# Four changes to where modulation products, first features and state products stand in a two-block transformer kernel

## The chip, the cores and the metric

One NeuronCore of a Trainium2 chip runs the whole program. The time is device microseconds of one execution. The profiler names the engines PE (TensorE matmul), PEld (its weight loads), DVE (VectorE), ACT (ScalarE), POOL (GpSimd) and SP (SyncE, which issues the DMAs). All engines work through their own queue in order. Everything is float32; a plain float32 product is two records on PE, a product of operands split in a high and a low part (fp32r) is one.

## The reference, cut to what matters

Two blocks of two layers each work on 512 tokens (256 of context, 256 latent) with 2048 features. Each layer begins with a modulation: a condition vector for the latent tokens and one for the context tokens goes through SiLU and a 2048 x 6144 matrix, which gives shift, scale and gate for every feature. The third layer holds a recurrent mixer (RWKV) with 16 heads of 64 in two directions.

```
shift, scale, gate = split(silu(c) @ mod_w[l] + mod_b[l], 3)      # for c and for c_ctx
h = norm(x) * (1 + scale) + shift
y = mixer(h)                # layer 1 sliding-window attention, 2 latent attention, 3 RWKV + pool, 4 attention
x = x + gate * y
# RWKV, per head, token by token:
sa = S @ a
S  = S * w + outer(sa, b) + outer(v, k)
y  = S @ r
```

## The kernel before

**Tiling.** Activations are kept with features on the partitions: 16 k-chunks of 128 features, 512 tokens wide. A layer's linear products stream weights through two buffers (`raw`, cut into `whi` and `wlo` by ACT and DVE, L323 and L324), and `mm3` multiplies each chunk three times (L352 to L354). The kernel text is Python that emits instructions; a scheduler then sets the order on each engine, by readiness as it reckons it and, among ready ones, by the place in the text. A block marked high priority goes ahead of all others as soon as it is ready.

**Modulation.** `mod_steps` (L244) is a generator that other work advances. One load is 1 MB: four k-chunks of 512 output features (`mraw`, L240). Its four products (L260, M = 32 columns of weights each) use four column strips of the array, `tile_position=(0, 32*j)`, and write four partition strips of one PSUM bank, `mv`; here they are called a group. There are 192 loads in all, 48 for each layer. After the last group of a batch ACT copies the bank (`ev`, L267), four products with a selection matrix add up the strips (L273), and DVE adds the bias (L279). For the first layer a batch is shift and scale of 512 features (8 loads), then all gates (16 loads); for the others a batch is 16 loads. `mod_open` sets how many load buffers there are: three in the stretches around the output projections and at the start, one inside the mixers (L706, L848, L977), so that there a load is issued only when the group before it has read the buffer.

**Start.** Two modulation loads are issued, then x in four DMAs (L1690); ACT squares, DVE sums them up (L1519 to L1523), PE and POOL make the inverse norm (`sums`, `spread`), and after the modulation of a group `scales` and `put_h` make four k-chunks of h. Between groups the key and value products of the first attention (`keys`, `values`) are advanced.

**Scan.** `rwkv` treats two heads at a time, one in each half of the partitions, in 8 chunks of 64 tokens; there are 16 such units. In each chunk, in one PSUM bank called `chain`: A times state (L1418), copy to `Rp` (L1421), Q times state (L1422), the inverse TT times `Rp` (L1428), copies into the state tile SV (L1429 DVE, L1430 ACT), BKs times SV (L1432), the new state (L1438, with SD from POOL), QB times SV added to Q's product (L1441), copy to y (L1444). A and Q lie in `AQ[:, c, 0]` and `AQ[:, c, 1]`, both heads side by side, and both are multiplied with both heads' states, 128 moving columns, of which half the products serve no one. Other units' preparation and the projections stand between these in PE's queue.

## Time and profile before

| | us |
|---|---|
| median of 3 runs (3293.38 to 3304.43) | 3296.71 |
| the profiled execution | 3288.34 |
| its span | 3286.3 |
| PE busy in the span | 3117.3 |
| DVE busy | 2101.0 |
| ACT busy | 1481.1 |

The table is read from the top: the profiled execution is 8.4 us under the median, and 2.0 us of it lie outside the span. PE is busy 95% of the span, the next engine 64%. A record's busy time overlaps with the next record's, so what one product costs in a full queue is the distance from its start to the next start, not its duration.

### The profile page before, as it was taken

Reading aid. Unit: us, or ns where it says so; the run is one execution under the profiler, and the core shown is the slowest. Engines: PE = TensorE matmul, PEld = TensorE weight load, DVE = VectorE, ACT = ScalarE, POOL = GpSimd, SP = SyncE. Lnnn points to the kernel's source line nnn. Section 1 sums busy time; section 2 is a strip of 40 time slices with the busy share of each in tenths; the row PEclk is TensorE's granted clock in tenths of the full one; section 3 lists DMA queues with packets and bytes.
Section 4 is the critical chain, followed back from the end, with each engine's and each line's share of the span. In section 5 each row is a group of like instructions: output and inputs, shape, how many; then the busy total and the mean of one; then the engine's idle time right before and its main releaser. Section 6 shows DMA issues by size and latency. Waiting matters only on the chain. (4 is left out here: it accounts for less than half of the span.)

```text
span 3286.3 us, 53227 instructions
## 1 busy us (share of the span) xinstructions
PE 3117.3 (95%) x19762; PEld 2397.2 (73%) x19762; DVE 2101.0 (64%) x4647; ACT 1481.1 (45%) x3233; POOL 351.2 (11%) x536
## 2 busy tenths in 40 slices
PE   5999999999988999999999999999999999899997
PEld 2567777767777788897776676666677768678897
DVE  2446454553376666666777788777787546857766
ACT  2424444442276666653334334333343323646664
POOL 0000000000001111000122222221121101200000
PEclk8999999999999999999999999999999999999999
DMA  8843444348654666766434433334434474543454
GB/s 303 309 165 135 139 137 157 125 174 290 234 165 142 226 208 226 253 228 211 126 98 133 124 125 116 111 103 149 126 109 154 168 253 130 172 140 129 143 180 153
DMA packets 270771, 556.07 MB, mean 169 GB/s; under 512 B 122928, under 2 KB 150704, under 8 KB 244912
## 3 DMA queue, kind: packets, MB, share of 16 engines
q1 hardware_dynamic: 270512, 552.68, 50.8%
q8 instruction: 155, 2.54, 0.3%
q14 instruction: 104, 0.85, 0.1%
HBM read 517.46 MB, written 35.13 MB: 168 GB/s over the span
## 5 line engine op out<-in xcount | busy, mean ns | idle before, releaser
L324 DVE TENSOR_TENSOR wlo<-raw,whi 128x512 fp32r<-128x512 f32 (+2 forms) x1000 | 660.3, 668 | 572.7 <-ACT whi L323 538.3
L352 PE MATMUL a<-hhi,whi 128*128 128x512 f32 (+1 forms) x2752 | 972.8, 355 | 16.6 <-ACT whi L323 11.9
L323 ACT CAST whi<-raw 128x512 fp32r<-128x512 f32 (+2 forms) x1000 | 593.0, 599 | 815.4 <-PE a L353 470.8
L353 PE MATMUL a<-hlo,whi 128*128 128x512 f32 (+1 forms) x2752 | 947.3, 345 | 0.0
L354 PE MATMUL a<-hhi,wlo 128*128 128x512 f32 (+1 forms) x2752 | 940.0, 347 | 4.5 <-DVE wlo L324 4.3
L352 PEld LDWEIGHTS a<-hhi,whi 128*128 128x128 f32 x2752 | 525.6, 191 | 145.2 <-issue 45.0
L354 PEld LDWEIGHTS a<-hhi,wlo 128*128 128x128 f32 x2752 | 522.6, 191 | 63.5 <-DVE wlo L324 10.2
L353 PEld LDWEIGHTS a<-hlo,whi 128*128 128x128 f32 x2752 | 526.3, 191 | 46.0 <-issue 2.2
L456 POOL TENSOR_TENSOR rs<-st,mhalf 128x4 f32<-128x4 f32 (+3 forms) x109 | 145.7, 1337 | 1683.3 <-DVE st L453 1666.3
L260 PE MATMUL mv<-mraw,cs 128*32 128x512 f32 x1536 | 258.3, 629 | 16.5 <-DMA mraw<-mod_w 16.2
L352 PE MATMUL a<-whi,hhi 128*128 128x512 f32 (+1 forms) x672 | 260.6, 398 | 13.4 <-ACT sq L613 5.9
L353 PE MATMUL a<-wlo,hhi 128*128 128x512 f32 (+1 forms) x672 | 262.7, 391 | 1.4 <-DVE wlo L324 1.1
L354 PE MATMUL a<-whi,hlo 128*128 128x512 f32 (+1 forms) x672 | 258.8, 388 | 0.0
L1427 POOL TENSOR_SCALAR SD<-SV,DL 64x64 f32<-64x64 f32 x224 | 130.0, 580 | 468.7 <-DVE SV L1438 452.4
L352 PEld LDWEIGHTS a<-whi,hhi 128*128 128x128 f32 x672 | 126.1, 190 | 71.2 <-issue 18.6
L353 PEld LDWEIGHTS a<-wlo,hhi 128*128 128x128 f32 x672 | 127.9, 190 | 31.5 <-DVE wlo L324 7.3
L354 PEld LDWEIGHTS a<-whi,hlo 128*128 128x128 f32 x672 | 127.6, 190 | 25.4 <-issue 0.8
L565 ACT ACTIVATE pr<-sc,nm 128x512 f32<-128x512 f32 (+1 forms) x128 | 81.1, 633 | 90.2 <-DVE nm L562 66.7
L1430 ACT COPY SV<-chain 64x64 f32<-64x64 f32 x128 | 26.6, 208 | 184.5 <-DVE SV L1429 178.8
L556 DVE TENSOR_REDUCE mx<-sc 128x1 f32<-128x512 f32 (+1 forms) x128 | 78.9, 617 | 37.8 <-PE sc L766 15.9
L260 PEld LDWEIGHTS mv<-mraw,cs 128*32 128x32 f32 x1536 | 37.0, 110 | 87.8 <-issue 50.3
L1444 ACT COPY y<-chain 64x64 f32<-64x64 f32 x256 | 52.9, 207 | 98.2 <-PE chain L1441 87.8
(379 smaller groups left out, 4690.6 us busy)
## 6 DMA issues: line engine op xcount, KB each, us to landing
mraw<-mod_w SPq DMA_DIRECT2D x192, 1024.0 KB, 4.9
raw<-od_in SPq DMA_DIRECT2D x88, 512.0 KB, 3.6
raw<-swa_in SPq DMA_DIRECT2D x72, 512.0 KB, 3.6
raw<-ev_rkv SPq DMA_DIRECT2D x64, 384.0 KB, 3.4
raw<-ev_in SPq DMA_DIRECT2D x48, 512.0 KB, 3.9
raw<-swa_out SPq DMA_DIRECT2D x40, 512.0 KB, 5.6
raw<-ev_out SPq DMA_DIRECT2D x40, 512.0 KB, 3.6
raw<-mla_g SPq DMA_DIRECT2D x64, 256.0 KB, 3.3
```

What stands on the lines that cost most here:

```text
L260: nc.tensor.matmul(pb[32 * j : 32 * j + 32, :], cs[:, 32 * k + 30 - 2 * n : 32 * k + 62 - 2 * n], raw[:, j, :], start=(n == 0 and q == 0), ...
L323: nc.scalar.copy(whi, raw)
L324: nc.vector.tensor_tensor(wlo, raw, whi.bitcast(F32), op=ALU.subtract)
L352: mm(out, ah, bh, start=first, stop=False, skip_group_check=shared)
L353: mm(out, ah, bl, start=False, stop=False, skip_group_check=shared)
L354: mm(out, al, bh, start=False, stop=last, skip_group_check=shared)
L456: self.nc.gpsimd.tensor_tensor(dst, stv, mv, op=ALU.pow)
L556: nc.vector.reduce_max(mx, sc, axis=AX.X)
L565: nc.scalar.activation(pr[:, :n], sc, AF.Exp, scale=scale, bias=nm, accum_out=sm)
L1427: nc.gpsimd.tensor_scalar(SD[r_], SV[r_, hh, c, :], DL[r_, c : c + 1], None, ALU.mult)
L1430: nc.scalar.copy(SV[half[1], 1, c, :], ps[half[1], P : P + L])
L1444: nc.scalar.copy(y[r_, c, :], blk(3 * P, hh))
```

## The change

Four parts. **(1) First layer in halves.** The modulation of the first layer's shifts and scales goes by 256 features in place of 512: a load is still 1 MB, now eight k-chunks of 256 features from a second layout of the weights, `mod_h`, and it takes eight products of 256 columns, two in each strip. A batch is four such loads in place of eight; `scales`, `put_h` and the key products follow each half, the values each second. At the start x is loaded first, then three modulation loads. **(2) Priority.** The products of a load stand in a high-priority block, for all 192 loads. **(3) Products per head.** `AQ[:, c, hh]` now holds A of one head and Q of that head, in swapped places for the second head, so that one product of 64 moving columns with its own head's state gives both. L1418 and L1422 (128 columns each) become two products of 64 columns, both ahead of the copy to `Rp`. QB, the mask and the final copies change places to match. **(4)** Even and odd chunks use two different column ranges of the bank `chain`; SD has one buffer in place of two.

```diff
@@ modulation
+MOD_FIRST = tuple(((g, u), (4 + g, u)) for g in range(4) for u in range(2)) + ((8, 9, 10, 11),)
+MOD_BATCHES = (0, 4, 1, 5), (2, 6, 3, 7), (8, 9, 10, 11)
...
-            self.nc.sync.dma_start(out=raw, in_=self.I["mod_w"][i, g, q])
+            if isinstance(g, tuple):
+                raw = raw.rearrange("p k (a c) -> p (k a) c", a=2)
+                self.nc.sync.dma_start(out=raw, in_=self.I["mod_h"][g[0], g[1], q])
+            else:
+                self.nc.sync.dma_start(out=raw, in_=self.I["mod_w"][i, g, q])
...
+                nq, nk, cols = (2, 8, 256) if half else (4, 4, 512)
...
-                        for j in range(4):
-                            k = 4 * q + j
-                            nc.tensor.matmul(
-                                pb[32 * j : 32 * j + 32, :], cs[:, 32 * k + 30 - 2 * n : 32 * k + 62 - 2 * n], raw[:, j, :],
-                                start=(n == 0 and q == 0), stop=(n == len(gs) - 1 and q == 3), tile_position=(0, 32 * j),
-                            )
+                        with self.tc.high_priority():
+                            for kk in range(nk):
+                                k, j = nk * q + kk, kk % 4
+                                nc.tensor.matmul(
+                                    pb[32 * j : 32 * j + 32, :cols], cs[:, 32 * k + 30 - 2 * n : 32 * k + 62 - 2 * n],
+                                    raw[:, kk, :], start=(n == 0 and k < 4), stop=(n == len(gs) - 1 and k >= KD - 4),
+                                    tile_position=(0, 32 * j),
+                                )
@@ rwkv
-            nc.vector.scalar_tensor_tensor(AQ[r_, :, 0, hh, :], ch(kkn)[r_], -1.0, Dp[r_, :, 0:L], ALU.mult, ALU.mult)
+            nc.vector.scalar_tensor_tensor(AQ[r_, :, hh, hh, :], ch(kkn)[r_], -1.0, Dp[r_, :, 0:L], ALU.mult, ALU.mult)
...
-            mm(ps[:, 0:P], heads(AQ[:, c, 0]), SV[:, :, c, :], start=True, stop=True)
+            o = c % 2 * P
+            for hh in range(2):
+                out = ps[:, o + hh * L : o + hh * L + L]
+                mm(out, heads(AQ[:, c, hh]), SV[:, hh, c, :], start=hh == 0, stop=False, skip_group_check=True)
...
-            mm(ps[:, 3 * P :], heads(AQ[:, c, 1]), SV[:, :, c, :], start=False, stop=False, skip_group_check=True)
             if not last:
-                SD = ph.tile([P, L], F32, tag="SD", name=self.nm("SD"), bufs=2)
+                SD = ph.tile([P, L], F32, tag="SD", name=self.nm("SD"), bufs=1)
...
-            mm(ps[:, 3 * P :], heads(QB[:, c]), SV[:, :, c, :], start=False, stop=True, skip_group_check=True)
+            mm(ps[:, o : o + P], heads(QB[:, c]), SV[:, :, c, :], start=False, stop=True, skip_group_check=True)
@@ tile_network
-        N.mod_load()
-        N.mod_load()
         for k4 in range(0, KD, 4):
             nc.sync.dma_start(out=x[k4 // 4], in_=I["x"][:, k4 : k4 + 4, :])
...
+        for _ in range(3):
+            N.mod_load()
...
-        for g in range(4):
+        for g, u in ((g, u) for g in range(4) for u in range(2)):
...
-            todo += [values(g)] * 16 + [kgen] * 16 if VF and g == 3 else [kgen] * 16 + [values(g)] * 16
+            todo += [kgen] * 8
+            if u:
+                todo += [values(g)] * 16
```

What it moves in the order that the scheduler sets is shown at three places on PE. In the changed kernel the lines are numbered 10 to 18 higher: groups are L270, `mm3` is L366 to L368, and the scan's products are L1437 (A and Q), L1446 (TT), L1450 (BKs) and L1459 (QB).

The start of the program on PE, before: `mv` with x4 is a group, L273 the adding up, `a` the key products. Ahead of these rows stand the inverse norm (`sums`, `spread`) and the first six groups.

```order
L260 MATMUL mv_188<-mraw_217,cs_185 32x512 x4
L260 MATMUL mv_188<-mraw_223,cs_185 32x512 x4
L273 MATMUL mv_38_237<-sel,ev_235 128x4 x4
L260 MATMUL mv_293<-mraw_229,cs_185 32x512 x4
L352 MATMUL a_274<-whi_280,hhi 128x512
L353 MATMUL a_274<-wlo_281,hhi 128x512
L352 MATMUL a_275<-whi_280,hhi 128x512
L353 MATMUL a_275<-wlo_281,hhi 128x512
```

The same place after, from the first group on (`spread` is the inverse norm, L284 the adding up):

```order
L270 MATMUL mv_190<-mraw_159,cs_187 32x256 x8
L488 MATMUL spread_174<-ident,rs_170 128x128 x2
L270 MATMUL mv_190<-mraw_161,cs_187 32x256 x8
L488 MATMUL spread_174<-ident,rs_170 128x128
L270 MATMUL mv_190<-mraw_163,cs_187 32x256 x8
L270 MATMUL mv_190<-mraw_207,cs_187 32x256 x8
L284 MATMUL mv_34_229<-sel,ev_227 128x4 x2
L270 MATMUL mv_269<-mraw_217,cs_187 32x256 x8
L366 MATMUL a_250<-whi_256,hhi 128x512
```

Moved: the adding up comes after four loads in place of eight, the first key product after five in place of nine, and the first groups stand among the transposes of `spread`. Behind these rows come 10 more key products, the sixth load's group, 10 more, and the seventh's; then the eighth's to eleventh's come with only 3 key products among them, ahead of the third k-chunk's products.

A chunk of the scan on PE, before, where a group is cut: one product of the load ahead of the chain's A product, three behind it.

```order
L1441 MATMUL chain_19159<-SV_18662,qb_14957 128x128
L260 MATMUL mv_17059<-mraw_19446,cs_9283 32x512
L1418 MATMUL chain_19159<-SV_18662,AQ_18258 128x128
L260 MATMUL mv_17059<-mraw_19446,cs_9283 32x512 x3
L352 MATMUL a_19063<-hhi,whi_19575 128x512
L353 MATMUL a_19063<-hlo,whi_19575 128x512
L354 MATMUL a_19063<-hhi,wlo_19576 128x512
L1422 MATMUL chain_19159<-SV_18662,AQ_18258 128x128
L1428 MATMUL chain_19159<-Rp_19490,tt 128x64
```

A chunk of the scan after: the four products of a load are one row (x4), and A and Q are two products of 64 columns that stand next to each other.

```order
L1437 MATMUL chain_21953<-SV_21456,AQ_21050 128x64 x2
L478 MATMUL sums_22213<-c_bsel,sq_22211 128x2 x4
L270 MATMUL mv_21434<-mraw_23186,cs_9552 32x512 x4
L1446 MATMUL chain_21953<-Rp_22168,tt 128x64
L366 MATMUL a_21857<-hhi,whi_22224 128x512
L367 MATMUL a_21857<-hlo,whi_22224 128x512
L368 MATMUL a_21857<-hhi,wlo_22225 128x512
L1450 MATMUL chain_21953<-SV_21456,BKs_21406 128x128
```

Moved: nothing stands between the products of a load, and nothing of the chain stands between `Rp` and TT. In the whole order before, 42 of the 192 groups are cut, 28 of them in the scan's layer; after, none is (160 rows with x4, 32 with x8).

What the chain's products wait for, before (`waits` names the engine whose semaphore it is):

```order
L1418 MATMUL chain_15808<-SV_15412,AQ_15210 128x128 [waits Activation_49]
L1280 MATMUL bon_15876<-r_15676,c_bones 128x512 [waits DVE_49,PE_49]
L352 MATMUL a_15573<-hhi,whi_15887 128x512
L1422 MATMUL chain_15808<-SV_15412,AQ_15210 128x128 [waits DVE_49]
L1428 MATMUL chain_15808<-Rp_15860,tt 128x64
L353 MATMUL a_15573<-hlo,whi_15887 128x512
L354 MATMUL a_15573<-hhi,wlo_15888 128x512
```

And after:

```order
L1459 MATMUL chain_15962<-SV_15566,qb_15110 128x128 [waits DVE_49]
L1295 MATMUL bon_16030<-r_15830,c_bones 128x512 [waits PE_49]
L1437 MATMUL chain_15962<-SV_15566,AQ_15364 128x64 [waits Activation_49]
L1437 MATMUL chain_15962<-SV_15566,AQ_15364 128x64
L366 MATMUL a_15727<-hhi,whi_16041 128x512
L367 MATMUL a_15727<-hlo,whi_16041 128x512
L368 MATMUL a_15727<-hhi,wlo_16042 128x512
L366 MATMUL a_15728<-hhi,whi_16041 128x512
L367 MATMUL a_15728<-hlo,whi_16041 128x512
L1446 MATMUL chain_15962<-Rp_16015,tt 128x64 [waits DVE_49]
```

Moved: the Q product is gone from between; the first product of a chunk waits for ACT as before.

## Rows read from the trace of the kernel before

**Rows 1.** The page: the span and how busy each engine is.

```profile
span 3286.3 us, 53227 instructions
PE 3117.3 (95%) x19762; PEld 2397.2 (73%) x19762; DVE 2101.0 (64%) x4647; ACT 1481.1 (45%) x3233; POOL 351.2 (11%) x536
```

**Rows 2.** Stretches: busy us of PE, PEld, DVE, ACT, POOL; then clock, DMA share, GB/s.

```profile
0.00:56.00 56.00, 19.51 (x92) 6.39 (x92) 16.09 (x30) 16.08 (x29) 2.19 (x8) 0.87 0.82 316
56.00:190.00 134.00, 129.71 (x647) 81.13 (x648) 57.84 (x111) 49.40 (x92) 2.03 (x2) 0.98 0.74 270
...
1460.00:2640.00 1180.00, 1140.48 (x7961) 814.35 (x7960) 881.35 (x2028) 446.67 (x1105) 234.71 (x416) 0.99 0.43 134
```

**Rows 3.** Instructions in order of time, start of the program: start us, us, engine, line.

```profile
25.97 1.83 PE L464 MATMUL sums<-ones,acc 128*128 128x2 f32 x8 [25.97 <-DVE acc L1523]
...
30.60 4.69 PE L260 MATMUL mv<-mraw,cs 128*32 128x512 f32 x24
...
48.89 1.94 PE L260 MATMUL mv<-mraw,cs 128*32 128x512 f32 x8 [2.17 <-DMA mraw<-mod_w]
...
56.33 0.80 PE L352 MATMUL a<-whi,hhi 128*128 128x512 f32 x1 [1.06 <-ACT hhi L498]
```

**Rows 4.** The same view, PE alone: a modulation group together, and one cut in two.

```profile
61.94 0.39 PE L353 MATMUL a<-wlo,hhi 128*128 128x512 f32 x1
62.17 0.40 PE L354 MATMUL a<-whi,hlo 128*128 128x512 f32 x1
62.49 1.07 PE L260 MATMUL mv<-mraw,cs 128*32 128x512 f32 x8
63.49 0.50 PE L352 MATMUL a<-whi,hhi 128*128 128x512 f32 x1
...
2000.31 1.05 PE L260 MATMUL mv<-mraw,cs 128*32 128x512 f32 x2
2001.29 0.49 PE L1418 MATMUL chain<-SV,AQ 128*128 128x128 f32 x2
2001.71 1.06 PE L260 MATMUL mv<-mraw,cs 128*32 128x512 f32 x6
2002.70 0.50 PE L352 MATMUL a<-hhi,whi 128*128 128x512 f32 x1
```

**Rows 5.** How long loads of modulation weights take, and what waits for them.

```profile
DMA to landing us min/median/max: 4.6/4.9/17.2
...
PE mv L260 <- DMA mraw<-mod_w: 8.8, 8, 4.1
```

**Rows 6.** PE in order of time, second attention: modulation groups close together.

```profile
1098.19 1.06 PE L260 MATMUL mv<-mraw,cs 128*32 128x512 f32 x8
1099.18 0.39 PE L352 MATMUL a<-hhi,whi 128*128 128x256 f32 x1
...
1104.25 1.07 PE L260 MATMUL mv<-mraw,cs 128*32 128x512 f32 x8
...
1259.50 0.38 PE L352 MATMUL a<-hhi,whi 128*128 128x256 f32 x1
...
1267.46 1.06 PE L260 MATMUL mv<-mraw,cs 128*32 128x512 f32 x8 [1.56 <-DMA mraw<-mod_w]
```

**Rows 7.** PE in order of time, inside the scan: products of 128, 64, 2 columns.

```profile
2003.50 0.38 PE L1422 MATMUL chain<-SV,AQ 128*128 128x128 f32 x2
2003.72 0.33 PE L1428 MATMUL chain<-Rp,tt 128*128 128x64 f32 x2
2003.86 0.48 PE L352 MATMUL a<-hhi,whi 128*128 128x512 f32 x1
...
2393.14 0.95 PE L464 MATMUL sums<-c_bsel,sq 128*128 128x2 f32 x8
2393.95 0.47 PE L352 MATMUL a<-hhi,whi 128*128 128x512 f32 x1
```

**Rows 8.** Who waits for whom in the scan, after 60 us: total us, times, longest us.

```profile
PEld chain L1418 <- ACT y L1444: 43.4, 86, 0.9
```

More of the change, by code (lines that the diff above doesn't have):

```diff
@@ L210, in modulation @@
         self.mod_done = set()
-        order = [(i, g) for i in range(4) for gs in MOD_BATCHES[min(i, 1)] for g in gs]
-        self.mod_loads = [(i, g, q) for i, g in order for q in range(4)]
+        order = [(i, g) for i in range(4) for gs in (MOD_BATCHES if i else MOD_FIRST) for g in gs]
+        self.mod_loads = [(i, g, q) for i, g in order for q in range(2 if isinstance(g, tuple) else 4)]
         self.mod_ahead, self.mod_pool, self.mod_wait = [], None, 0
@@ L248, in mod_steps @@
             mod, cs = self.mod[i], self.cs
-            for gs in MOD_BATCHES[min(i, 1)]:
+            for gs in MOD_BATCHES if i else MOD_FIRST:
                 pb = self.bank("mv")
+                half = isinstance(gs[0], tuple)
+                nq, nk, cols = (2, 8, 256) if half else (4, 4, 512)
                 for n, g in enumerate(gs):
-                    for q in range(4):
+                    for q in range(nq):
                         while len(self.mod_ahead) < (self.mod_pool[1] - 1 if self.mod_pool and self.mod_loads else 0):
@@ L270, in mod_steps @@
                 p2 = self.bank("mv2")
-                c = 2 * len(gs)
-                for j in range(4):
+                c, nb = 2 * len(gs), cols // P
+                for j in range(nb):
                     nc.tensor.matmul(
@@ L276, in mod_steps @@
                 for n, g in enumerate(gs):
-                    bias = self.v("mod_b", i * 48 + g * 4, 4).unsqueeze(2).broadcast_to([P, 4, 2])
-                    pv = p2[:, : 4 * c].rearrange("p (j n c) -> p j n c", j=4, c=2)[:, :, n, :]
-                    nc.vector.tensor_tensor(mod[:, g * 4 : (g + 1) * 4, :], pv, bias, op=ALU.add)
+                    o = g[0] * 4 + g[1] * 2 if half else g * 4
+                    bias = self.v("mod_b", i * 48 + o, nb).unsqueeze(2).broadcast_to([P, nb, 2])
+                    pv = p2[:, : nb * c].rearrange("p (j n c) -> p j n c", j=nb, c=2)[:, :, n, :]
+                    nc.vector.tensor_tensor(mod[:, o : o + nb, :], pv, bias, op=ALU.add)
                     self.mod_done.add((i, g))
+                    if half and g[1]:
+                        self.mod_done.add((i, g[0]))
                 yield
@@ L1088, in ev_consts @@
         nc.gpsimd.memset(self.smask[:, 0:NT:L], 0.0)
-        self.gmask = load("gmask", [P, P])
+        self.gmask = load("gmask", [P, 3 * L])
         self.m16 = load("m16", [P, 64])
@@ L1251, in rwkv @@
             r_ = half[hh]
[L1252 removed]
+            nc.vector.tensor_tensor(AQ[r_, :, hh, 1 - hh, :], ch(r)[r_], Dp[r_, :, 1:], op=ALU.mult)
         yield
@@ L1269, in rwkv @@
                     lhs = BK[r_, c, :, :].rearrange("p a t -> p (a t)")
-                    mm(pbs[hh][:, (c - c4) * P : (c - c4 + 1) * P], lhs, AQ[r_, c, :, hh, :], start=True, stop=True)
+                    mm(pbs[hh][:, (c - c4) * P : (c - c4 + 1) * P], lhs, AQ[r_, c, hh], start=True, stop=True)
             for hh in range(2):
@@ L1427, in rwkv @@
                     nc.gpsimd.tensor_scalar(SD[r_], SV[r_, hh, c, :], DL[r_, c : c + 1], None, ALU.mult)
-            mm(ps[:, P : P + L], heads(TT[:, c]), Rp, start=False, stop=True, skip_group_check=True)
-            nc.vector.tensor_copy(SV[half[0], 0, c, :], ps[half[0], P : P + L])
-            nc.scalar.copy(SV[half[1], 1, c, :], ps[half[1], P : P + L])
+            mm(ps[:, 3 * P : 3 * P + L], heads(TT[:, c]), Rp, start=False, stop=True, skip_group_check=True)
+            nc.vector.tensor_copy(SV[half[0], 0, c, :], ps[half[0], 3 * P : 3 * P + L])
+            nc.scalar.copy(SV[half[1], 1, c, :], ps[half[1], 3 * P : 3 * P + L])
             if not last:
@@ L1473, in rwkv @@
             for hh in range(2):
-                r_, src = half[hh], pv[half[hh], :, hh * L : (hh + 1) * L]
+                r_, src = half[hh], pv[half[hh], :, L - hh * L : 2 * L - hh * L]
                 to = ch(yf)[r_, (hh + c0) % 2 :: 2, :]
@@ L1745, in tile_network @@
                     owed -= 1.0
-                    if not all((0, i) in N.mod_done for i in (g, 4 + g)):
+                    if not all((0, (i, u)) in N.mod_done for i in (g, 4 + g)):
                         next(N.side["mod"][0])
-            N.need(0, (g, 4 + g))
-            N.scales(mod[0], N.v("norm_g", 0, KD), s0, 4 * g, 4 * g + 4)
-            for k in range(4 * g, 4 * g + 4):
+            N.need(0, ((g, u), (4 + g, u)))
+            k0 = 4 * g + 2 * u
+            N.scales(mod[0], N.v("norm_g", 0, KD), s0, k0, k0 + 2)
+            for k in range(k0, k0 + 2):
                 t = N.t512("xr")
@@ L2014, in layout @@
     A["bsel"] = (i[:, None] // 64 == np.arange(2)[None, :]).astype(f32)
-    A["gmask"] = np.concatenate([l[:, None] < t[None, :], l[:, None] <= t[None, :]], axis=1).astype(f32)
+    low = l[:, None] < t[None, :]
+    A["gmask"] = np.concatenate([low, l[:, None] <= t[None, :], low], axis=1).astype(f32)
     A["m16"] = ((l[:, None] // 32 == t[None, :] // 32) & (l[:, None] // 16 < t[None, :] // 16)).astype(f32)
```

22 lines of the change are left out of this document (11 added, 11 removed).

## The prediction

> **What bounds the kernel now.** I read the page's busy times first: PE is busy 3117 us of a span of 3286, the next engine 64% [rows 1]. By stretches it is the same picture everywhere but at the start: from 0 to 56 us PE does 19.5 us of work, from 56 to 190 it does 129.7 of 134, and in the scan 1140 of 1180 [rows 2]. So behind 56 us the time is the work in PE's queue plus what PE waits there in order, and ahead of it the time is a chain of loads. The order of time at the start shows the chain: x's sums reach PE at 25.97, the first group follows at 30.60, the eighth runs at 48.89, and the first key product starts at 56.33 [rows 3]. That all modulation groups before it wait behind the sums comes from PE's order in the section on the change.
>
> What one piece costs on a full PE I take from start to start. A split product of 512 columns costs 0.23 us (61.94 to 62.17), and a modulation group whose four products stand together 1.00 (62.49 to 63.49) [rows 4].
>
> **The change part by part.**
>
> *Start.* x is issued ahead of the loads, so two loads of 1.05 MB no longer stand before it. At the 316 GB/s of this stretch [rows 2] that is 6.6 us; I take 5.9, since ACT and DVE must still work through x. The sums reach PE at about 20.1, and the first group follows them by 4.6 us as now (25.97 to 30.60) [rows 3], at 24.7, when three loads have landed. The fourth load needs the first group's buffer, free near 26.7 (the granted clock of this stretch is 0.87 in the mean, between the levels of 1.2 and 2.4 GHz; the group at 48.89 took 1.94, and I take that); it lands 4.9 us after its issue [rows 5], and its group ends at 33.5. From the end of the eighth group to the first key product it is 56.33 - 50.83 = 5.5 us now [rows 3], so the first key product can start at 39, 17 us earlier. That is the upper bound. The lower one: the third k-chunk's products stand behind the eleventh load, and seven more loads at 3.3 us (1.05 MB at 316 GB/s) put it at 55. At 56 us PE has then done 24 key products (5.5 us) and two groups (2.0) more than today, 8 us. Further on loads and work run at about the same rate, so I keep near the low end: **-10 us**, between -17 and -5. A load's eight products are two rounds of half the columns on the same four strips. One product of 512 columns alone keeps PE 0.98 us [rows 4], one of 128 columns 0.22 [rows 7]: the price goes by columns here, and I keep 1.00 for a group. If each round paid the whole 1.00, the 32 loads would cost 32 us more, a bound that these two rows speak against. More additions, scales and `ev` copies of half the size lie on DVE and ACT, which are idle for more than half of this stretch [rows 2].
>
> *Groups that stay together.* Where a group is cut, PE runs one product alone, on one strip: it keeps PE from 2000.31 to 2001.29, 0.98 us, and the other three take 0.99 more, 2001.71 to 2002.70 [rows 4]. Together they cost 1.00. A cut so costs 0.97 us of PE's own time. The order of before cuts 42 groups, that of after none: 42 x 0.97 = 41 us. This is PE work, and no engine hides it, but in the scan PE also waits for the chain behind a cut: the first product of a chunk finds ACT's copies late 86 times, 43.4 us in all [rows 8], and part of the second run covered such waits. I give the 14 cuts outside the scan their full 13.6 us and the 28 in it two thirds, 18 of 27: **-32 us**, between -14 and -41.
>
> *Groups pulled forward.* The other side of priority is that a group stands in PE's queue as soon as the scheduler believes its load to be there. Inside the mixers there is one load buffer, so the next load is issued when the last group has read it. Counted in the order by the prices above, 66 of the 123 groups there now have only 5 to 6 us of PE work between them and the group before; today 10 have. If the load is late then, PE stops, and everything behind the group stops with it; SP's queue, in which the next load waits for that group, holds back the weight loads behind it too. Two pairs bound the price. After 1099.18 the next group starts at 1104.25, 5.07 us later, without a wait of note. After 1259.50 the next starts at 1267.46, and PE has idled 1.56 us [rows 6]: 7.96 us, some 2.4 more than a close group has. I take one close group in eight to be like the second: 66 x 0.3 = 20 us, less the 8.8 us that PE waits for loads today behind 60 us [rows 5]: **+11 us**. The bounds are -9 (all land in time) and +60 (about half are late by 2.4, less those 9, and nothing runs meanwhile).
>
> *Products per head.* In each of 128 chunks two products of 128 columns become two of 64; all are two records. The row of 128 columns takes 2003.50 to 2003.72, 0.11 a record; records with only 2 columns against 128 x 128 weights take 0.10 (eight from 2393.14 to 2393.95) [rows 7]. So the moving columns do not set the pace here, something that 2 and 128 columns share does, and a record of 64 columns lies between. Four records save at most 4 x 0.01 = 0.04 us, 5 us in all. The chain gets two records more ahead of `Rp` (+0.2 us) and two fewer between `Rp` and TT (-0.2). **-5 us**. The upper bound is the 64-column row itself, 0.14 for two records right behind others (2003.72 to 2003.86): 4 x 0.04 x 128 = 20 us less. The lower one, a wait of 0.1 us more in each chunk, is +13.
>
> The Trainium skill, "TensorE: Matmul & The Clock Gate", section "LDWEIGHTS (loading the stationary operand)", gives P / 1.2 ns for P weight columns, 107 ns for 128, in line with the 0.10; its section "Back-to-back issue gap" gives N / 2.4 + 2.5 ns for an isolated matmul, by which half the columns would be half the price. By that rule the saving would be an estimated 2 x 0.11 x 128 = 28 us in place of 5.
>
> *Two column ranges, one SD buffer.* They look as if a chunk's first product need no longer wait for y's copies. Today that product writes columns 0 to 127 of the bank and y is read from 384 on, and still it waits 86 times for that copy [rows 8]; after, the same product still waits for ACT's semaphore. **0 us**; were the wait gone, up to -43. SD's next value needs the state that the last reader of SD makes, so one buffer adds nothing while only one unit's chain runs.
>
> The Trainium skill, "PSUM — Partial Sum Buffer", section "PSUM bank collisions raise a hardware error", asks for a semaphore by bank and quadrant, not by address. That fits the row: by that rule the two ranges free nothing.
>
> The sum is -10 - 32 + 11 - 5 + 0 = -36 us: 3288.3 becomes 3252. The median stands 8.4 us over the profiled execution, and I add it: **3261 us**.
>
> **The rivals.** *All of it comes.* Loads land in time (-9 in place of +11), all cuts count (-41), the start brings 14 and the narrow products 10: -74, so 3223. For it: PE is full by every stretch. Against it: the close spacing above. Chance 0.25. If half the columns were half the price, it is this case too, 3238 with the rest as forecast.
>
> *The chain keeps it.* In the scan PE waits in order; if DVE and ACT set the pace there, its 28 cuts give nothing, the start brings 8, the 14 other cuts 13.6, and the waits cost 20: about 0, 3296. For it: DVE is busy 881 of 1180 us in the scan [rows 2]. Against it: PE does 1140 of 1180. Chance 0.14.
>
> *Groups ahead of their loads.* Each close group stops PE. Without this term the change brings 47 us, so it decides once the 66 wait 0.85 us each on average ((47 + 9) / 66); at 1.3 us they cost 86 - 9 = 77, and the time is 3327. For it: one buffer, and a load takes up to 17.2 us [rows 5]. Against it: the median is 4.9, and the spacing is 5 to 6. Chance 0.09.
>
> **How the numbers follow.** The forecast has 0.52. Two measurements of this kernel tell 0.3% apart, 10 us. Faster by more than that: all of the forecast but 0.04, the first rival, 0.03 of the second: 0.76. Within it: 0.04 and 0.08 of the second: 0.12. Slower: the third rival and the 0.03 left: 0.12. The range reaches from the first rival, a little under it for its own bounds, to just short of no change: 3217 to 3292; it leaves out the slow rival and half of the second.
>
> **What would show it.** In the changed kernel's trace the first key product starts near 39 us, PE's third k-chunk near 55, and the stretch to the end of the values is 10 us shorter. No group of PE is cut; groups' busy time falls by some 40 us. PE's waits for modulation loads behind 60 us are near 20 us and lie in the attention stretches. The pair of 64-column products costs as much from start to start as one pair of records of 128 (0.2 us each). The first product of a chunk still waits for ACT. The forecast is wrong if those waits for loads are over 50 us, or if PE's idle time in the scan grows by as much as the cuts gave back.

## The result, and the profile after

The changed kernel takes **3321.3 us** (median; 3317.3 to 3325.0) against 3296.1 for the kernel before, a ratio of 1.0067 with a 95% interval of 1.0043 to 1.0091. It is slower by some 22 us; 3261 was predicted, with a range of 3217 to 3292. The profiled execution has a span of 3318.5 us against 3286.3 [rows 1].

The page of the changed kernel: the span, busy time of each engine, the modulation groups (busy us, mean ns, idle ahead and what ended it), and the loads (KB, median us to landing).

```profile
span 3318.5 us, 53812 instructions
...
PE 3106.2 (94%) x20018; PEld 2417.7 (73%) x20018; DVE 2102.7 (63%) x4663; ACT 1481.5 (45%) x3237; POOL 382.6 (12%) x536
...
L270 PE MATMUL mv<-mraw,cs 128*32 128x512 f32 (+1 forms) x1792 | 213.5, 566 | 42.9 <-DMA mraw<-mod_w 36.4
...
mraw<-mod_w SPq DMA_DIRECT2D x160, 1024.0 KB, 5.7
...
mraw<-mod_h SPq DMA_DIRECT2D x32, 1024.0 KB, 7.5
```

PE is busy 11 us less than before, yet the span is 32 us longer: PE's idle time (span less busy time) went from 169 to 212 us. The groups' own work fell as it should, from 258.3 us on the page of before (1536 records) to 213.5. So 45 us of work went, only 11 of them show in PE's busy time, and 43 us of waiting came.

What PE waits for behind 60 us (total us, times, longest us), to compare with [rows 5]:

```profile
PE mv L270 <- DMA mraw<-mod_w: 36.4, 32, 3.4
...
PE yt L1489 <- DVE y L1478: 7.6, 6, 3.0
...
PE yt L1489 <- ACT Z L1410: 6.6, 6, 1.5
```

The missing 34 us are the clock. The mean granted clock of TensorE and the span, by core, of the changed kernel and of the kernel before:

```profile
core 0: 3318.5 us, clock 0.973
```

```profile
core 0: 3286.3 us, clock 0.983
```

At 0.973 of full speed the execution loses (1 - 0.973) x 3318.5 = 90 us, at 0.983 of 3286.3 it is 56. The lower of the two levels, 1.2 GHz, is granted oftener (the stretches in which it is are called half-clock spells below), and whatever PE does then takes longer. This gives an account that adds up for all kernels below: span = work at full clock + idle time + time lost to the clock (an upper bound, since a waiting PE loses nothing; counted only where PE is busy it is 71 us in the change and 48 in the eleventh run, so the rest is some 15 us too low, by about as much in each row).

| profiled execution | span | PE idle | lost to the clock | rest: work |
|---|---|---|---|---|
| before | 3286 | 169 | 56 | 3061 |
| the change | 3319 | 212 | 90 | 3017 |
| priority alone (first run) | 3316 | 210 | 83 | 3023 |
| three of four (fifth run) | 3259 | 179 | 59 | 3021 |
| all four outside the scan (ninth run) | 3286 | 193 | 72 | 3021 |
| the start with three (tenth run) | 3265 | 176 | 72 | 3017 |
| the change with three (eleventh run) | 3250 | 173 | 62 | 3016 |
| a second load buffer (twelfth run) | 3280 | 197 | 56 | 3027 |

All kernels without cut groups do 34 to 46 us less work. They differ by 70 us in what they wait and at which clock.

### The profile page after: what moved, and what is told of

It reads as the page before. It is cut to its first block, busy times and chain, and to the rows that moved or that the text cites. A ratio compares the mean times of both kernels' runs of the same rounds, so it can differ in the third digit from the quotient of the medians.

```text
span 3318.5 us, 53812 instructions
## 1 busy us (share of the span) xinstructions
PE 3106.2 (94%) x20018; PEld 2417.7 (73%) x20018; DVE 2102.7 (63%) x4663; ACT 1481.5 (45%) x3237; POOL 382.6 (12%) x536
## 5 line engine op out<-in xcount | busy, mean ns | idle before, releaser
L366 PE MATMUL a<-hhi,whi 128*128 128x512 f32 (+1 forms) x2752 | 971.1, 354 | 16.8 <-ACT whi L337 7.5
L368 PE MATMUL a<-hhi,wlo 128*128 128x512 f32 (+1 forms) x2752 | 945.5, 349 | 8.1 <-DVE wlo L338 7.8
L366 PEld LDWEIGHTS a<-hhi,whi 128*128 128x128 f32 x2752 | 527.5, 192 | 97.0 <-issue 23.5
L368 PEld LDWEIGHTS a<-hhi,wlo 128*128 128x128 f32 x2752 | 524.3, 192 | 81.0 <-issue 17.5
L367 PEld LDWEIGHTS a<-hlo,whi 128*128 128x128 f32 x2752 | 528.3, 192 | 62.4 <-issue 17.8
L366 PE MATMUL a<-whi,hhi 128*128 128x512 f32 (+1 forms) x672 | 259.8, 396 | 15.0 <-ACT whi L337 5.9
L368 PE MATMUL a<-whi,hlo 128*128 128x512 f32 (+1 forms) x672 | 260.9, 391 | 0.0
L270 PE MATMUL mv<-mraw,cs 128*32 128x512 f32 (+1 forms) x1792 | 213.5, 566 | 42.9 <-DMA mraw<-mod_w 36.4
L1445 POOL TENSOR_SCALAR SD<-SV,DL 64x64 f32<-64x64 f32 x224 | 159.7, 713 | 548.8 <-DVE SV L1456 517.7
L366 PEld LDWEIGHTS a<-whi,hhi 128*128 128x128 f32 x672 | 126.1, 190 | 52.3 <-ACT whi L337 8.5
L368 PEld LDWEIGHTS a<-whi,hlo 128*128 128x128 f32 x672 | 128.1, 191 | 31.7 <-issue 7.9
L270 PEld LDWEIGHTS mv<-mraw,cs 128*32 128x32 f32 x1792 | 40.3, 110 | 108.5 <-DMA mraw<-mod_w 53.8
L1440 DVE COPY Rp<-chain 64x64 f32<-64x64 f32 x256 | 56.7, 221 | 92.3 <-PE chain L1437 81.5
L1437 PEld LDWEIGHTS chain<-SV,AQ 128*128 128x128 f32 x512 | 71.1, 194 | 52.1 <-ACT y L1462 44.2
```

The lines of the kernel that those rows point to most:

```text
L270: nc.tensor.matmul(pb[32 * j : 32 * j + 32, :cols], cs[:, 32 * k + 30 - 2 * n : 32 * k + 62 - 2 * n], raw[:, kk, :], start=(n == 0 and k < ...
L366: mm(out, ah, bh, start=first, stop=False, skip_group_check=shared)
L367: mm(out, ah, bl, start=False, stop=False, skip_group_check=shared)
L368: mm(out, al, bh, start=False, stop=last, skip_group_check=shared)
L1437: mm(out, heads(AQ[:, c, hh]), SV[:, hh, c, :], start=hh == 0, stop=False, skip_group_check=True)
L1440: nc.vector.tensor_copy(Rp[half[hh]], blk(o, hh))
```

## The experiments

Each is told with its ratio to the kernel before, run on the same chip; the kernel before had medians from 3290 to 3298 there. A median and a ratio of the same run can differ by some us.

**First run: high priority alone.** To the kernel before only this is added:

```
-                        for j in range(4):
+                        with self.tc.high_priority():
+                          for j in range(4):
```

> The kernel before with one part of the change: the four products of a modulation group under high priority. Before is 3296 us. Theory A (priority costs more than it gives: loads are waited for, and in the scan the chain loses the work that stood in its gaps, so PE waits there and its granted clock falls): the groups' busy time falls from 258 to about 214 us, PE's waits for modulation loads rise to over 30, half-clock spells in the scan rise from 31 us to over 80, and the time is 3315 to 3340. Theory B (the scan's products per head and the new column ranges cost it): spells as before, time 3265 to 3285. Theory C (the three parts only cost together): 3290 to 3300.

Measured: 3316.8 us, ratio 1.0071 (1.0054 to 1.0087). The page's busy times and groups, and PE's longest wait behind 60 us:

```profile
PE 3105.6 (94%) x19762; PEld 2407.9 (73%) x19762; DVE 2103.2 (63%) x4647; ACT 1481.7 (45%) x3233; POOL 346.9 (10%) x536
...
L261 PE MATMUL mv<-mraw,cs 128*32 128x512 f32 x1536 | 216.7, 641 | 43.2 <-DMA mraw<-mod_w 42.9
...
PE mv L261 <- DMA mraw<-mod_w: 35.2, 35, 4.1
```

Priority alone makes the whole loss. Theory A holds in every number but one: the half-clock spells of the scan came to 58 us, not over 80.

**Second run: the change without priority.**

```
-                        with self.tc.high_priority():
+                        if True:
```

> The changed kernel without high priority: the start by halves and the scan's products per head stay. Theory A (priority is the cost): the granted clock in the scan is 0.99 as before, PE's waits for modulation loads behind 60 us are near 10 us, groups are cut again (busy near 258), and the time is 3275 to 3290, the start's gain. Theory B (the scan's part is the cost): 3300 to 3320, with half-clock spells of over 80 us in the scan. Theory C (only together): 3285 to 3296.

Measured: 3295.0 us, ratio 0.9997 (0.9978 to 1.0017). Start and scan together neither gain nor lose anything that can be measured. The time is 5 us over theory A's range and inside theory C's; but theory C has no single part lose alone, and priority did. Theory B falls. Two more signs of theory A failed: PE's waits for modulation loads behind 60 us are 15.2 us, not near 10, and the scan is granted 0.97, not 0.99, its half-clock spells being 61 us against 31 before. The scan's stage:

```profile
1578.00:2613.00 1035.00, 1001.37 (x7115) 713.50 (x7114) 795.03 (x1868) 395.72 (x1008) 235.07 (x381) 0.97 0.42 126
```

**Third run: the start alone** (the diff's parts on loads by halves, `x` ahead of the loads and the keys by pairs of k-chunks; scan as before, no priority).

```
+        for _ in range(3):
+            N.mod_load()
...
+        for g, u in ((g, u) for g in range(4) for u in range(2)):
```

> The kernel before with the start alone: x ahead of the loads, the first modulation by 256 columns, the keys of a k-chunk pair after each. The forecast for this part was -10 us (-17 to -5), so 3286; the first key product near 38 us in place of 56. If the start's lead is only waited away later (the values stand behind the same weight loads, or the modulation's remaining groups are later), the time is 3293 to 3298, though the first key product still starts near 38.

Measured: 3290.8 us, ratio 0.9991 (0.9979 to 1.0002), so -3 us (-7 to +1). The median lies between the forecast's 3286 and the 3293 to 3298 of a lead that is waited away. PE in order of time:

```profile
38.61 1.65 PE L366 MATMUL a<-whi,hhi 128*128 128x512 f32 x3 [1.85 <-ACT whi L337]
```

The first key product starts 18 us earlier than in [rows 3]. Counted at ACT's casts of weight tiles, which come in the same order in both kernels, this lead is 13 us at the eleventh cast and 6.7 at the twenty-first (192.3 against 199.0 us), between 4 and 7 at the casts beside it; up to there PE has idled 36.6 us in place of 43.7.

**Fourth run: the scan alone** (products per head, column ranges, one SD buffer).

```
+            for hh in range(2):
+                out = ps[:, o + hh * L : o + hh * L + L]
+                mm(out, heads(AQ[:, c, hh]), SV[:, hh, c, :], start=hh == 0, stop=False, skip_group_check=True)
```

> The kernel before with the scan's part alone: products per head of 64 moving columns, two column ranges, one SD buffer. The forecast for this part was -5 us (-20 to +13), so 3291. Theory A (priority is the cost of the change) expects 3280 to 3296 with a granted clock of 0.99 in the scan. Theory B (this part is the cost) expects 3305 to 3325, the granted clock in the scan near 0.96 and PE's idle time there larger.

Measured: 3298.1 us, ratio 1.0002 (0.9984 to 1.002). This part is not the cause of the loss. The time is 2 us over theory A's range and 7 under theory B's. In the profiled execution (3308 us, next to the slowest of ten) the scan is granted 0.97, where theory A expected 0.99, though PE idles no longer there than before (36 us against 38):

```profile
1587.00:2624.00 1037.00, 1000.82 (x7111) 715.26 (x7110) 794.39 (x1866) 395.60 (x1007) 230.40 (x381) 0.97 0.41 125
```

**Fifth run: priority on three of the four.** The first product of a group keeps the place it had, and the other three follow it at once.

```
                         for j in range(4):
+                          with self.tc.high_priority() if j else ExitStack():
```

> The kernel before, with high priority on the second, third and fourth product of a group alone. The first takes its place as before, the others follow it at once: no group is cut (as with priority on all four), and the groups stand where they stood before. Theory A1 (groups that stand ahead of their loads are the cost, and uncut groups are worth what the forecast says): waits for modulation loads behind 60 us stay near 9 to 15 us, the groups' busy time is near 215, and the time falls by 20 to 35 us, to 3261 to 3276. Theory A2 (an uncut group saves nothing on the chip: the cut's second run stood in PE's waits and kept the granted clock up): the groups' busy time falls as much, but the time stays at 3290 to 3302, with more half-clock spells in the scan than the 31 us of before.

Measured: **3261.6 us, ratio 0.9898 (0.9864 to 0.9933)**, 34 us under the kernel before. Its page and its longest wait behind 60 us:

```profile
PE 3079.8 (95%) x19762; PEld 2390.8 (73%) x19762; DVE 2100.7 (64%) x4647; ACT 1478.6 (45%) x3233; POOL 347.1 (11%) x536
...
L261 PE MATMUL mv<-mraw,cs 128*32 128x512 f32 x1536 | 213.2, 631 | 23.1 <-DMA mraw<-mod_w 23.1
...
PE mv L261 <- DMA mraw<-mod_w: 14.3, 9, 4.2
```

The groups cost as little as in the first run, and no group is cut in either. The one difference in the text is the first product's priority, and so where a group stands; it is worth 55 us (3316.8 less 3261.6). Uncut groups are worth what the forecast gave them; groups pulled forward cost more than they save. Theory A1 holds.

**Sixth run: all four, but in the scan's stage alone.**

```
+                        with self.tc.high_priority() if self.scan else ExitStack():
```

> The kernel before with high priority on groups only while the scan's stage is open (its one-buffer ring); the attention stages and the stretches between keep the old order. Theory A1 (standing ahead of loads costs, mostly in the attention stages): waits for loads rise by under 8 us, the scan's 28 cuts are gone, the time is 3280 to 3292. Theory A2 (the scan needs its cut groups): 3305 to 3318, with half-clock spells in the scan of 50 us or more; the rest of the +20 of priority alone lies in the attention stages if this run is below 3306.

Measured: 3298.5 us, ratio 1.0004 (0.9987 to 1.0021), between the two theories' ranges. PE's waits for loads are 17.1 us, 8 more than before; the scan's half-clock spells are 65 us, over the 50 that theory A2 named. What the uncut groups save in the scan (the groups' busy time falls from 258 to 230 us), pulling them forward there takes away again.

**Seventh and eighth run: a quarter of each load.** In both kernels three quarters of the modulation weights are left out.

```
-            self.nc.sync.dma_start(out=raw, in_=self.I["mod_w"][i, g, q])
+            self.nc.sync.dma_start(out=raw[:, 0:1, :], in_=self.I["mod_w"][i, g, q, :, 0:1, :])
```

> Priority alone, as in the first run, but each modulation load brings a quarter (the first 512-column row of its four, and all four products read it): loads of 262 KB land early. What is left out: three quarters of the modulation weights, so the output is another. If waiting for loads is what priority costs, the waits fall from 35 to under 8 us and the time to 3265 to 3285 (less what the smaller traffic gives by itself, which the next run measures). If the order in the scan and the clock cost it, loads or not, the difference to the next run stays at +15 to +25 us.

> The kernel before with the same quarter loads (three quarters of the modulation weights left out, the output is another), as the base for the run ahead of it. The start's chain of loads shortens by up to 20 us (eight loads of 1.05 MB to a quarter at 316 GB/s, partly behind x's own 4 MB), and the 9 us of waits for loads behind 60 us go: 3262 to 3285. By the theory that waits for loads are the cost of priority, priority with quarter loads is then 10 to 35 us faster than this; by the theory of order and clock it is 15 to 25 slower.

Measured: 3279.7 with priority (ratio 0.9953, 0.9936 to 0.9971) and 3262.0 without (0.9894, 0.9859 to 0.9929). Priority still costs 18 us, inside the 15 to 25 of the theory of order and clock. PE's waits for modulation loads behind 60 us, with priority and then without:

```profile
PE mv L261 <- DMA mraw<-mod_w: 24.4, 39, 2.8
```

```profile
PE mv L260 <- DMA mraw<-mod_w: 11.3, 11, 2.1
```

Against what I had expected, the waits did not go with the smaller loads: there are more of them (39 against 35), each shorter. The reason stands in the order of the seventh run. The scheduler knows how large a load is, and with priority it puts the group as close behind the last one as it believes the load to allow: in the two attention stages 64 of 71 groups now have less than 5 us of PE work between them and the group before, where the first run's order has 5 to 6 us in 49 places. The traces agree: between 190 us and the scan 91 of 103 groups stand so close in the seventh run, and 18 of 107 in the first. So the run does not take the loads' lateness away, and can't be read as a price of the order without it. It shows that smaller loads alone don't cure groups under priority.

**Ninth run: three of four in the scan, all four outside it.**

```
+                          with self.tc.high_priority() if j or not self.scan else ExitStack():
```

> As the fifth run (no group cut, 3262 us), but outside the scan's stage all four products of a group have high priority, so that the groups of the attention stages stand close behind each other again (5 to 6 us of PE work in 49 places); in the scan the first product keeps its place. It splits the 55 us between the fifth run and the first: if all of it were waits for loads, which lie mostly in the attention stages, this run stands at 3300 to 3317; if it lies in the scan's lost gap work, at 3262 to 3275; by the stages of the two traces (13 us of the difference by the first mixer, 25 by the end of the second, the rest in the scan) it stands near 3290.

Measured: 3287.6 us, ratio 0.996 (0.9942 to 0.9978). Of the 55 us between the fifth and the first run, 26 come from priority outside the scan (3287.6 less 3261.6) and 29 from priority in it, near what the stages of the traces had said; by the ratios to the kernel before, which allow for the three chips, it is 20 and 37. The profiled spans of the ninth and fifth run differ by 27.0 us: 14 of idle time (the waits for loads rise from 14.3 to 31.9) and 13 to 14 of clock, by the table. Some 5 us of that clock lie in the scan, where both runs set the same priorities and idle equally (39 and 40 us), so they are not shown to come from the groups outside.

**Tenth and eleventh run: the start with three of four, and the whole change with three of four.** In both the priority stands as in the fifth run; the eleventh differs from the changed kernel in this alone:

```
-                        with self.tc.high_priority():
-                            for kk in range(nk):
-                                k, j = nk * q + kk, kk % 4
+                        for kk in range(nk):
+                            k, j = nk * q + kk, kk % 4
+                            with self.tc.high_priority() if kk else ExitStack():
```

> The start's part together with priority on all products of a group but its first; the scan as before. If the parts add, it is the fifth run's 3262 less the 5 to 7 us that the start alone gave (its median and its trace at the end of the values): 3254 to 3258. If the start's lead only moves a wait, 3260 to 3264.

> The changed kernel with one difference: the first product of a group keeps its place, the others follow it with priority. If the pulled-forward groups are the whole reason why the change lost, this is the forecast that the change missed: near 3258, and at least 25 us under the kernel before. If the scan's products per head cost something next to uncut groups, 3262 to 3275; it stands above 3290 only if the change's other parts lose together with priority.

Measured: 3261.4 us (0.9879, 0.9858 to 0.9901) and **3254.6 us (0.9863, 0.9842 to 0.9884)**. The eleventh beats both kernels: 44 us under the one before, 67 under the change (by the ratios, 1.0067 - 0.9863 = 0.0204 of 3296), as expected if the pulled-forward groups are the reason. The tenth's median lies where the start's lead only moves a wait; it is not told apart from the fifth, nor the eleventh from the tenth; what start and scan add to it stays within a few us.

**Twelfth run: a second load buffer in the second attention stage**, otherwise the ninth.

```
-            self.mod_open(ph, 1, PACE[2])
+            self.mod_open(ph, 2, PACE[2])
```

> As the ninth run (priority on all four products outside the scan, 3288 us), with two load buffers in place of one in the second attention stage, where the ninth run's PE waits 11.5 us for loads, 9 times. With two loads under way the scheduler's order puts 30 of the 36 groups there less than 5 us of PE work behind the group before. If a single buffer is the reason for the waits, they fall below 4 us and the time falls by 5 to 12, to 3276 to 3283. If priority puts a group wherever the scheduler believes its load landed, and the real load is later than that, one buffer or two, the waits there stay at 8 us or rise to 25, and the time is 3285 to 3305.

Measured: 3275.8 us, ratio 0.9952 (0.9932 to 0.9972). PE's waits for loads from 960 to 1330 us, in the ninth run and in this one:

```profile
PE mv L262 <- DMA mraw<-mod_w: 11.5, 9, 2.6
```

```profile
PE mv L262 <- DMA mraw<-mod_w: 6.3, 6, 1.6
```

Inconclusive. The waits halve and don't vanish, between what either reading wanted; the median is 12 us under the ninth's, at the edge of the first reading's range, but the kernel before was 8 us faster beside this run too, and the intervals of the two ratios overlap.

## Why the prediction was wrong, point by point

**The start, -10.** Right in its mechanism, too large in size. PE in order of time in the changed kernel:

```profile
21.19 1.84 PE L478 MATMUL sums<-ones,acc 128*128 128x2 f32 x8 [21.19 <-DVE acc L1541]
...
24.86 1.94 PE L270 MATMUL mv<-mraw,cs 128*32 128x256 f32 x16
...
37.56 1.20 PE L366 MATMUL a<-whi,hhi 128*128 128x512 f32 x4 [2.32 <-ACT whi L337]
...
45.33 1.07 PE L270 MATMUL mv<-mraw,cs 128*32 128x256 f32 x16
46.33 0.50 PE L366 MATMUL a<-whi,hhi 128*128 128x512 f32 x1
...
56.31 2.07 PE L366 MATMUL a<-whi,hhi 128*128 128x512 f32 x4 [0.86 <-ACT whi L337]
```

The sums were forecast at 20.1, the first group at 24.7, the first key product at 39, the third k-chunk near 55; they stand at 21.19, 24.86, 37.56 and 56.31. A load's sixteen records of 256 columns take 1.00 us from start to start (45.33 to 46.33), as priced. What is left near the end of the stage in the third run's trace, 6.7 us, lies within the term's bounds; what is left in the time, 3 us (-7 to +1), is below the smaller of them, 5.

**Groups that stay together, -32.** Right. The fifth run does this and nothing else: -34. The full 41 us of the bound came as work (groups 258.3 to 213.2; PE's busy time fell by 37.5), and 10 us of it went back into idle time (169 to 179). The two thirds for the scan had meant to cover such waits, but PE's idle time in the scan grew by only 2 of these 10 us (38 to 40): size right, place of the discount not.

**Groups pulled forward, +11.** This is the step that failed. The eleventh run is the change with this one thing undone, and it is 67 us faster; in the kernel before, without the other parts, the same step is worth 55 (first run against fifth). So the term was +55 to +67, at or above its own upper bound of +60, and not +11. By the table the 67 are 39 us of idle time and 28 of clock, and the forecast priced one part of them, the waits for loads.

*The waits for loads* were forecast at 20 us and are 36.4. One close group in eight was to be late by 2.4 us; in fact 32 waits average 1.1. Against the eleventh run's 17.8 that is 19 us of the 67. The prediction held a median landing of 4.9 us against a spacing of 5 to 6. With the groups pulled forward the landing itself is longer, 5.7 us on the changed kernel's page above; in the eleventh run it is not:

```profile
mraw<-mod_w SPq DMA_DIRECT2D x160, 1024.0 KB, 5.0
```

*The clock*, which the forecast left out. In the second attention stage of the changed kernel, PE in order of time, and then two stretches of the same place (busy us by engine, then the granted clock):

```profile
1108.85 0.28 PE L367 MATMUL a<-wlo,ckh 128*128 128x256 f32 x1
1110.72 1.94 PE L270 MATMUL mv<-mraw,cs 128*32 128x512 f32 x8 [1.59 <-DMA mraw<-mod_w]
1112.59 0.58 PE L368 MATMUL a<-whi,ckl 128*128 128x256 f32 x1
```

```profile
1104.00:1110.00 6.00, 4.70 (x38) 4.29 (x36) 5.23 (x13) 3.29 (x7) 0.64 (x2) 1.00 0.75 253
1110.60:1114.00 3.40, 3.28 (x14) 1.62 (x15) 1.70 (x4) 0.00 (x0) 0.56 (x1) 0.50 0.29 42
```

PE waits 1.59 us for the load, the granted clock falls to 0.50 (1.2 GHz in place of 2.4), and the group that was waited for takes 1.87 us to the next instruction instead of 1.00. By the table 90 against 62 us are lost to the clock, 28 us of the 67; over all four executions of each kernel it is 94 against 68. But such places do not make the difference. From 60 us to the scan, where most loads are waited for, the half-clock spells are 51 us in the change and 48 in the eleventh run; in the scan they are 92 against 38, and there the waits for loads are 2.7 us. So in the change the late loads do not explain the clock that was lost. The stretch from 60 us to the scan in the change and in the eleventh run:

```profile
60.00:1604.00 1544.00, 1459.94 (x8883) 1137.50 (x8881) 844.44 (x1871) 723.84 (x1543) 78.21 (x98) 0.98 0.58 195
```

```profile
60.00:1569.00 1509.00, 1448.93 (x8848) 1133.52 (x8846) 843.60 (x1870) 723.01 (x1543) 78.46 (x98) 0.98 0.58 197
```

In the kernel before it is otherwise: there priority raises the spells from 34 to 56 us ahead of the scan and from 41 to 58 in it (fifth and first run). No run changed the clock alone, and what sets it is not shown. Idle time does not by itself: the second and fourth run, whose PE idles 34 and 36 us in the scan against 38 before, have 61 and 65 us of spells there against 31.

*The scan*, also left out. Idle time rises by 39 us between the eleventh run and the change; 19 are waits for loads, 12 are other waits in the scan, and 8 are other waits elsewhere. The scan's stage (first to last state product) is 34 us longer than in the eleventh run, half of the 67. The stage's row in the change and in the eleventh run:

```profile
1604.00:2640.00 1036.00, 984.73 (x7061) 717.76 (x7062) 790.73 (x1859) 395.55 (x1004) 251.07 (x381) 0.96 0.41 121
```

```profile
1569.00:2571.00 1002.00, 964.10 (x7092) 695.70 (x7090) 790.96 (x1861) 393.88 (x1003) 237.15 (x381) 0.98 0.42 129
```

PE idles 13 us more in it (51 against 38), and most of the rest is the lower clock. One place where such a wait begins is the end of a unit, where the transposes `yt` wait for DVE's `y` and ACT's `Z`. PE there in the eleventh run, and at the same step of the changed kernel:

```profile
2392.49 1.15 PE L1395 MATMUL inv<-t,Z 64*64 64x64 f32 x32
2393.57 1.07 PE L270 MATMUL mv<-mraw,cs 128*32 128x512 f32 x8
2394.57 0.98 PE L1489 MATMUL yt<-ident,y 128*128 128x128 f32 x7
```

```profile
2455.68 1.15 PE L1395 MATMUL inv<-t,Z 64*64 64x64 f32 x32
2459.86 1.09 PE L1489 MATMUL yt<-ident,y 128*128 128x128 f32 x4 [3.03 <-DVE y L1478]
2461.97 0.90 PE L1489 MATMUL yt<-ident,y 128*128 128x128 f32 x3 [1.02 <-ACT Z L1410]
```

and the stretch that follows in the changed kernel:

```profile
2459.00:2469.00 10.00, 6.51 (x47) 4.54 (x47) 9.28 (x15) 3.55 (x7) 1.03 (x3) 0.50 0.20 79
```

Without priority on its first product a group is what the scheduler has left when nothing else is ready, so it lands in such gaps: ahead of 11 of the 16 units' `yt` in the fifth run and 7 in the eleventh, but of only 2 in the first run and 2 in the changed kernel (counted where a group is among PE's nine records ahead). There it has run earlier, beside work that would have kept PE busy anyway. That the lost filling of gaps is what costs the scan its time is argued, not shown. The waits at `yt` behind 60 us, in the first run and in the fifth:

```profile
PE yt L1472 <- ACT Z L1396: 4.1, 6, 1.4
PE yt L1472 <- DVE y L1461: 3.4, 3, 1.7
```

```profile
PE yt L1472 <- ACT Z L1396: 5.8, 4, 1.5
PE yt L1472 <- DVE y L1461: 5.4, 5, 2.4
```

They are shorter in the first run (7.5 us against 11.2), where nearly all the groups are gone from that place, and in the changed kernel they are only some 4 us longer than in the eleventh run; the rest of the 12 is spread over other products. The forecast had asked what a pulled-forward group waits for, and neither what the place that it left was doing there nor which clock PE would be granted.

**Products per head, -5.** Right within its bounds; the fourth run measures 0 (-5 to +7). In the changed kernel the four 64-column records of a chunk take 0.39 us from start to start:

```profile
2004.26 0.56 PE L1437 MATMUL chain<-SV,AQ 128*128 128x64 f32 x4
2004.65 1.08 PE L1295 MATMUL bon<-r,c_bones 128*128 128x512 f32 x2
```

In the mean of all chunks it is 0.48 us against 0.55 for the two pairs of 128 columns before, 0.07 x 128 = 9 us of work. So half the columns are nowhere near half the price here. The estimate of 28 us worked out from the Trainium skill ("TensorE: Matmul & The Clock Gate", section "Back-to-back issue gap", N / 2.4 + 2.5 ns) is not borne out: the measured saving is a third of it. The section gives that rule for an isolated matmul and says itself that in a stream of weight loads and matmuls it under-counts at small N, which fits these rows: at 128 columns a record takes 0.11 us [rows 7], where the rule gives an estimated 0.056. The work that was saved does not show in the time; in the fourth run's profiled execution the scan's lower clock (0.97 against 0.99) takes more than it. POOL's scaling of the state, no part of the sum, takes 159.7 us in place of 130.0; none of DVE's waits in either trace ends on it.

**Column ranges and SD, 0.** Right. The first product of a chunk still waits for ACT's copies of y, 93 times ([rows 8]: 86 times, 43.4 us):

```profile
PEld chain L1437 <- ACT y L1462: 44.2, 93, 0.9
```

The Trainium skill's "PSUM — Partial Sum Buffer", section "PSUM bank collisions raise a hardware error", asks for a semaphore by bank and quadrant; this row, two column ranges with the same wait, agrees.

**The rivals.** "Groups ahead of their loads" named 3327, and the time is 3321, but not by its mechanism alone. It was to decide at 0.85 us of waiting per close group; the waits rose by 36.4 - 8.8 = 27.6 us over 66 groups, 0.42 each, half of that, and the change still lost. "The chain keeps it" was right that the scan would give nothing back, but put that on the cuts, where it belongs to the groups' places: the fifth run has no cuts, and its scan idles only 2 us more. The sum without the failed term, -47, is close to what the eleventh run gives, -44, but in part by luck: measured alone, the start, the uncut groups and the products per head give -3, -34 and 0, together -37.

**The signs of being wrong.** Neither of the two that the prediction named appeared. The waits for loads are 36.4 us, not over 50, and PE's idle time in the scan grew by 13 us, not by the 27 that its cuts were reckoned at. The forecast was still 60 us off, because neither sign looks at the clock and each looks at one part alone.

**What stays open.** Why the scan of the kernels under priority is granted the lower clock oftener, and how much of the scan's loss is lost filling of gaps. How much would remain if the loads alone were in time: the seventh and the twelfth run were to show it, and neither took the waits away. Whether the start or the scan's products add anything to uncut groups is below what these rounds tell apart.

## What to carry to other kernels

Separate the two things that a priority does: keeping instructions together, and moving them forward. Where only the first is wanted, leave the first instruction its place and give priority to those that follow it; here that is the difference between +22 and -44 us. When filler work is moved, price the place that it leaves as well as the one it goes to, and read the granted clock stage by stage beside the waits: here it holds 28 of the 67 us at most, and a forecast from waits alone does not see it.

## What the runs showed of the hardware that was not expected

The lower level of TensorE's clock can cost as much as the waits, and it differs between kernels that do the same work. The uncut kernels of the table do the same work within 12 us, and the time lost to the clock runs from 56 to 90 us. In the fifth, ninth and first run it rises with PE's idle time (59, 72 and 83 us lost at 179, 193 and 210 us idle), but the tenth (72 at 176) and the twelfth (56 at 197) do not follow, so no price of the clock per us of waiting can be read from these traces. One kernel differs from execution to execution too: over 25 executions the kernel before was granted 0.978 to 0.985, which is 73 to 49 us lost.

Modulation loads landed later when their groups were pulled forward: 5.7 us in the median in the change and in the first run, 5.0 in the eleventh and the fifth, 4.9 before, with the same number of bytes. A landing time read from the kernel before is no bound for the kernel after.
